# One load of 128 partitions in place of five for the first row tile of a matmul-trace kernel

## The chip, the cores and the metric

The kernel runs on one core of a Trainium2 chip. A core has a matrix engine (TensorE, PE in the profile), three engines for elementwise work (VectorE = DVE, ScalarE = ACT, GpSimd = POOL), SyncE (SP), which here only issues transfers, and 16 DMA engines that move data between the chip's memory (HBM) and the core's on-chip memory (SBUF, 128 partitions). The metric is the device time of one execution in microseconds (us). Where several runs are shown, it is their median.

## The reference

Two stacks of eight 2176 x 2176 float32 matrices are given. For each of the eight pairs the trace of the product is wanted.

```
B, N = 8, 2176
prod = np.matmul(a, b)
traces = np.diagonal(prod, axis1=1, axis2=2).sum(axis=-1)
```

The trace of a product needs no matrix product: it is the sum over i and k of a[i,k] times b[k,i]. So the work is one elementwise product of b with the transpose of a, summed. Both stacks have to be read once, 303 MB in all; there are few operations per byte.

## The kernel before

A matrix is cut into 17 row tiles of 128 rows (`NT`). GpSimd loads them with its own DMA queue, which casts float32 to bfloat16 on the way (`load`, L68 to L78, issue in L76). A load takes eight row tiles at a time (two groups of four, 4352 KB as written), or one single row tile (544 KB). The large loads go to the pool `stage` of three buffers, the single ones to `single` of two. With 17 tiles a matrix takes two large loads and one single one.

Per batch, matrix a is loaded and transposed on TensorE, 128 x 128 at a time (L158 and L179), into PSUM; `evacuate` copies the results into the tile `at`, two of three copies on ScalarE (L115), one on VectorE (L113). Then matrix b is loaded, and VectorE multiplies its rows with the matching rows of `at` and sums in one instruction (`multiply_reduce`, L125). The products of a batch are held behind VectorE's last copy of that batch (`tc.issue_after(copies_end.ins)`, L239). In the last batch a part of the products goes to TensorE (`pe_work`, L286), and the last row tile comes in three pieces (`LAST_PIECES`, L250). At the end VectorE reduces what TensorE has summed, a matmul with ones adds up the partitions, and SyncE writes out eight numbers (L306).

Instructions of one engine run in the order of the program. A load waits for the last reader of the buffer that it overwrites: a large load of a for the transposes of the tile before in that buffer, a large load of b for VectorE's products with the old one.

The first row tile of the first batch is different. It is the single row tile of a (the last 128 rows of the matrix), and is put first in the order of loads. Here `load_first` (L80 to L90) has SyncE load it as float32, without a cast, into the words of a buffer of `stage`. ScalarE casts the left half (L88) and VectorE the right half (L89) into a bfloat16 tile. After this function is called, the first large load of a is issued on GpSimd ahead of the constants (`ahead`, L222), and the identity matrices and other constants follow. The buffer with the float32 words is one of the three of `stage`, so GpSimd's third large load (the first of b) waits until both casts have read it.

The float32 tile is 128 rows of 8704 bytes, 1.11 MB. `FIRST_SPLIT` (L45) cuts it by partitions into five loads:

```
FIRST_SPLIT = [(0, 96), (96, 104), (104, 112), (112, 120), (120, 128)]
```

They are issued one after the other by SyncE (L86, L87). Both casts need all five.

Of the kernel before, what the change touches and what calls it, by code (L numbers as in the profile page):

```python
# [20 lines left out]
def kernel(  # L21
# [6 lines left out]
    nc = tc.nc  # L28
    P = 128
# [12 lines left out]
    a_groups = row_groups(P, even)  # L42
    DOUBLE = 2

    FIRST_SPLIT = [(0, 96), (96, 104), (104, 112), (112, 120), (120, 128)]  # L45

    LAST_PIECES = [(0, 2), (2, 3), (3, 5)]

    const = ctx.enter_context(tc.tile_pool(name="const", bufs=1))
# [30 lines left out]
    def load_first(src, start):  # L80

        words = stage.tile([P, DOUBLE * ROWS, N], bf16, tag="stage")
        plain = words.bitcast(f32).rearrange("p r k -> p (r k)")[:, :N]
        half = N // 2
        t = single.tile([P, 1, N], bf16, tag="single")
        for lo, hi in FIRST_SPLIT:  # L86
            nc.sync.dma_start(out=plain[lo:hi, :], in_=src[start + lo:start + hi, :])  # L87
        nc.scalar.copy(out=t[:, 0, :half], in_=plain[:, :half])  # L88
        nc.vector.tensor_copy(out=t[:, 0, half:], in_=plain[:, half:])  # L89
        return [(start, 1, t)]  # L90
# [119 lines left out]
    for bi in range(BATCH):  # L210
# [8 lines left out]
        for start, m, count in loads:  # L219
            if not tiles:  # L220
                groups = load_first(a[bi], start)
                ahead, issued = load(a[bi], *loads[1])  # L222
                with tc.issue_after(issued.ins):
                    constants()
            elif ahead is not None:
                groups, ahead = ahead, None
            else:
                groups, _ = load(a[bi], start, m, count)
            for start, m, a_t in groups:
                last_transpose = transpose_group(at, a_t, start, m, b_groups)  # L230
# [12 lines left out]
        for start, m, count in joined(b_groups):  # L243
            if last and start == N - P:
# [3 lines left out]
                for g0, g1 in LAST_PIECES:  # L248
                    lo, hi = g0 * WIDE, min(g1 * WIDE, N)
# [29 lines left out]
            out=tiles["sums"][:, bi:bi + 1], in_=acc[:, :cols], axis=mybir.AxisListType.X  # L279
# [4 lines left out]
    with tc.issue_after(last_transpose.ins):  # L284
        for n, (x, y) in enumerate(pe_work):
            nc.tensor.matmul(  # L286
                trace_ps, x, y, start=(n == 0), stop=(n == len(pe_work) - 1),
            )
    late_acc = tiles["late"]
    for n, (x, y) in enumerate(late):  # L290
# [6 lines left out]
        start=True, stop=True,  # L297
    )
    parts = [tiles["sums"][:, BATCH - 1:BATCH]] + [late_acc[:, n:n + 1] for n in range(len(late) + 1)]
    for n, part in enumerate(parts):  # L300
        nc.tensor.matmul(  # L301
            total[:, BATCH - 1:BATCH], tiles["ones"], part,
            start=(n == 0), stop=(n == len(parts) - 1),
# [3 lines left out]
        out=out.rearrange("(a b) -> a b", a=1),  # L307
        in_=tiles["result"][:1, :BATCH],
# [31 lines left out]
```

## Time and profile before

| what | value |
|---|---|
| median of 3 runs | 714.15 us (713.23 to 714.8) |
| the profiled execution | 714.8 us |
| its span, first to last instruction | 713.0 us |
| DVE busy | 411.5 us, 58% of the span |
| PE busy | 206.7 us, 29% |
| ACT busy | 196.9 us, 28% |
| POOL busy | 34.6 us, 5% |
| bytes read from HBM | 303.04 MB, 425 GB/s over the span |
| bytes written by the transfers | 152.32 MB, mean 214 GB/s |

The profile comes from one execution with the hardware profiler on. Its time is 1.8 us above its span: what lies before the first and after the last instruction. Reads are about twice the written bytes because nearly all loads cast four bytes to two. Each line of a timeline has a start, a duration, the engine, the line of the kernel, the operation, what it writes and reads, and in brackets how long the engine was idle before and what ended that. "Landing" of a transfer is the moment at which the engine that waits for it sees it. The trace also holds a record for each DMA packet, with start, duration, queue and bytes written; it does not name the DMA engine that moved it. An instruction queue is a queue by which an engine's program is fetched; it uses the same DMA engines.

Of the transfers, the page lists 16 large loads of a and 15 of b, all issued by GpSimd, with a median of 47.2 and 49.9 us from issue to landing, and for SyncE one load of 816 KB (9.9 us to landing) and four of 68 KB.

### The profile page before, as it was taken

Reading aid. Unit: us, or ns where it says so; the run is one execution under the profiler, and the core shown is the slowest. Engines: PE = TensorE matmul, PEld = TensorE weight load, DVE = VectorE, ACT = ScalarE, POOL = GpSimd, SP = SyncE. Lnnn points to the kernel's source line nnn. Section 1 sums busy time; section 2 is a strip of 40 time slices with the busy share of each in tenths; the row PEclk is TensorE's granted clock in tenths of the full one; section 3 lists DMA queues with packets and bytes.
Section 4 is the critical chain, followed back from the end, with each engine's and each line's share of the span. In section 5 each row is a group of like instructions: output and inputs, shape, how many; then the busy total and the mean of one; then the engine's idle time right before and its main releaser. Section 6 shows DMA issues by size and latency. Waiting matters only on the chain.

```text
span 713.0 us, 3721 instructions
## 1 busy us (share of the span) xinstructions
PE 206.7 (29%) x1406; PEld 193.2 (27%) x1406; DVE 411.5 (58%) x449; ACT 196.9 (28%) x210; POOL 34.6 (5%) x60
## 2 busy tenths in 40 slices
PE   0344005430054200633006420054100651006655
PEld 0344005430054200533006410054100550005545
DVE  0023996229961399514995149942499325993356
ACT  1355003440054300534006330064200652006610
POOL 1000000000000000000001000000000000000000
PEclk9987555775567755767557775576755766557775
DMA  9999999999999999999999999999999999999996
GB/s 195 218 218 215 215 215 217 219 219 209 223 215 216 216 215 222 216 216 216 216 217 218 218 217 216 212 220 217 216 219 212 221 218 216 216 215 219 217 211 122
DMA packets 11652, 152.32 MB, mean 214 GB/s; under 512 B 882, under 2 KB 1138, under 8 KB 3314
## 3 DMA queue, kind: packets, MB, share of 16 engines
q0 software_dynamic: 11456, 150.97, 99.7%
q1 hardware_dynamic: 178, 1.11, 0.7%
q8 instruction: 11, 0.18, 0.1%
q14 instruction: 7, 0.06, 0.0%
HBM read 303.04 MB, written 0.00 MB: 425 GB/s over the span
## 4 chain that ended last, share of the span: by engine, by line
DMA 60%; DVE 31%; issue 7%; PE 2%; DVEq 0%; another core or an unknown queue 0%; POOLq 0%
DMA t<-in_b_dram 50%; DVE scratch L125 30%; DMA t<-in_a_dram 11%; PE ps L158 2%; DVE acc L125 0%; DVEq L125 0%; PE ps L179 0%; PE total L301 0%; DVE result L305 0%; DVE late L125 0%; POOLq L76 0%; DVE sums L278 0%; POOLq L324 0%
## 5 line engine op out<-in xcount | busy, mean ns | idle before, releaser
L125 DVE CUSTOM_DVE_ANT_1 scratch<-at,t 128x2048 bf16<-128x2048 bf16 (+1 forms) x156 | 310.6, 1991 | 73.7 <-DMA t<-in_b_dram 66.4
L115 ACT COPY at<-ps 128x1024 bf16<-128x1024 bf16 x208 | 194.5, 1045 | 467.7 <-PE ps L158 467.6
L158 PE MATMUL ps<-identity,t 128*128 128x128 f32 x1071 | 178.3, 333 | 485.3 <-DMA t<-in_a_dram 310.0
L158 PEld LDWEIGHTS ps<-identity,t 128*128 128x128 f32 x1071 | 166.4, 213 | 493.8 <-DVE sums L278 365.6
L113 DVE COPY at<-ps 128x1024 bf16<-128x1024 bf16 (+2 forms) x104 | 93.6, 902 | 210.1 <-PE ps L158 190.7
L76 POOL DMA_DIRECT2D t<-in_a_dram x23 | 15.3, 663 | 352.9 <-PE ps L179 156.8
L76 POOL DMA_DIRECT2D t<-in_b_dram x26 | 16.8, 646 | 293.0 <-PE ps L179 142.0
L286 PEld LDWEIGHTS <-at 128*128 128x128 bf16 x153 | 17.3, 125 | 13.6 <-issue 13.0
L286 PE MATMUL trace_ps<-t,at 128*128 128x128 bf16 x144 | 16.7, 294 | 12.6 <-DMA t<-in_b_dram 12.6
L179 PE MATMUL ps<-identity,t 128*128 128x128 bf16 x170 | 16.4, 219 | 5.0 <-DVE at L113 4.7
L179 PEld LDWEIGHTS <-t 128*128 128x128 bf16 x170 | 13.0, 100 | 8.4 <-issue 8.2
L125 DVE DVE_READ_ACCUMULATOR2_ANT acc<- 128x1 f32 x163 | 13.3, 82 | 0.0
L89 DVE CAST t<-words 128x1088 bf16<-128x1088 f32 x1 | 0.7, 727 | 13.9 <-DMA words<-in_a_dram 13.9
L88 ACT ACT_TABLE_LOAD x1 | 1.3, 1283 | 14.7 <-DMA words<-in_a_dram 14.7
L250 POOL DMA_DIRECT2D b_t<-in_b_dram x3 | 1.6, 537 | 16.4 <-DVE acc L125 16.4
L125 DVE CUSTOM_DVE_ANT_0 scratch<-at,t 128x128 bf16<-128x128 bf16 x7 | 2.0, 291 | 0.2
L125 DVE CUSTOM_DVE_ANT_1 scratch<-at,b_t 128x256 bf16<-128x256 bf16 (+1 forms) x3 | 1.5, 510 | 0.1
L278 DVE TENSOR_REDUCE sums<-acc 128x1 f32<-128x22 f32 (+1 forms) x8 | 1.4, 174 | 0.3
L286 PE MATMUL trace_ps<-b_t,at 128*128 128x128 bf16 x9 | 1.3, 286 | 0.4 <-DMA b_t<-in_b_dram 0.4
L88 ACT CAST t<-words 128x1088 bf16<-128x1088 f32 x1 | 1.1, 1097 | 0.0
L301 PE MATMUL total<-late,ones 128*1 128x1 f32 x8 | 0.8, 164 | 0.8 <-DVE late L125 0.8
L301 PEld LDWEIGHTS total<-late,ones 128*1 128x1 f32 x8 | 0.3, 80 | 1.2 <-DVE late L125 1.2
(14 smaller groups left out, 2.7 us busy)
## 6 DMA issues: line engine op xcount, KB each, us to landing
t<-in_a_dram POOLq DMA_DIRECT2D x16, 4352.0 KB, 47.2
t<-in_b_dram POOLq DMA_DIRECT2D x15, 4352.0 KB, 49.9
t<-in_b_dram POOLq DMA_DIRECT2D x9, 544.0 KB, 54.4
t<-in_a_dram POOLq DMA_DIRECT2D x7, 544.0 KB, 53.1
t<-in_b_dram POOLq DMA_DIRECT2D x1, 2176.0 KB, 42.3
t<-in_b_dram POOLq DMA_DIRECT2D x1, 1088.0 KB, 26.1
words<-in_a_dram SPq DMA_DIRECT2D x1, 816.0 KB, 9.9
words<-in_a_dram SPq DMA_DIRECT2D x4, 68.0 KB
```

Source lines behind the costliest of these rows:

```text
L76: issued = nc.gpsimd.dma_start(out=part, in_=rows)
L88: nc.scalar.copy(out=t[:, 0, :half], in_=plain[:, :half])
L89: nc.vector.tensor_copy(out=t[:, 0, half:], in_=plain[:, half:])
L113: last_copy = nc.vector.tensor_copy(out=dst, in_=src)
L115: nc.scalar.copy(out=dst, in_=src)
L125: nc.vector.tensor_tensor_reduce(out=out, in0=x, in1=y, scale=1.0, scalar=0.0, op0=MUL, op1=ADD, accum_out=acc,)
L158: nc.tensor.transpose(ps[:, n * m + r, :], words[:, r, c0:c0 + step * (P - 1) + 1:step], tiles[f32],)
L179: last_transpose = nc.tensor.transpose(ps16[:, n, r, :], a_t[:, r, c0:c0 + P], tiles[bf16],)
L250: nc.gpsimd.dma_start(out=row[:, lo:hi], in_=b[bi, start:start + P, lo:hi])
L278: nc.vector.reduce_sum(out=tiles["sums"][:, bi:bi + 1], in_=acc[:, :cols], axis=mybir.AxisListType.X)
L286: nc.tensor.matmul(trace_ps, x, y, start=(n == 0), stop=(n == len(pe_work) - 1),)
L301: nc.tensor.matmul(total[:, BATCH - 1:BATCH], tiles["ones"], part, start=(n == 0), stop=(n == len(parts) - 1),)
```

## The change

The list `FIRST_SPLIT` and its loop go. SyncE issues one load of all 128 partitions. The tile, its buffer, the casts that read it and all else stay as they are.

```diff
-    FIRST_SPLIT = [(0, 96), (96, 104), (104, 112), (112, 120), (120, 128)]
-
     LAST_PIECES = [(0, 2), (2, 3), (3, 5)]
 ...
         t = single.tile([P, 1, N], bf16, tag="single")
-        for lo, hi in FIRST_SPLIT:
-            nc.sync.dma_start(out=plain[lo:hi, :], in_=src[start + lo:start + hi, :])
+        nc.sync.dma_start(out=plain, in_=src[start:start + P, :])
         nc.scalar.copy(out=t[:, 0, :half], in_=plain[:, :half])
         nc.vector.tensor_copy(out=t[:, 0, half:], in_=plain[:, half:])
```

## The prediction

> **What bounds the kernel now.** I read the page's slices and queues first, then the chain that ended last, then the timeline of the first 20 us and of the last 10, and last the trace's records of single DMA packets.
>
> The page (slices: busy tenths, then GB/s; queues: packets, MB, share of 16 engines):
>
> ```profile
> span 713.0 us, 3721 instructions
> DMA  9999999999999999999999999999999999999996
> q0 software_dynamic: 11456, 150.97, 99.7%
> q1 hardware_dynamic: 178, 1.11, 0.7%
> ```
>
> The 16 DMA engines are full from the first slice to the next to last. GpSimd's queue q0 (every load but the first) has work 99.7% of the time; q1 is SyncE's queue, and nearly all of it is the load that the change touches. So the bound is the transfer itself, and a change can only count where it alters when the DMA engines finish. DVE, the busiest compute engine, has 58%.
>
> The end of the chain (start, us, what), and the same place in the timeline:
>
> ```profile
> 677.29 26.12 DMA t<-in_b_dram
> 703.44 0.05 DVEq L125
> ```
>
> ```profile
> 703.45 0.82 PE L286 MATMUL trace_ps<-t,at 128*128 128x128 bf16 x6 [3.50 <-DMA t<-in_b_dram]
> 703.57 2.29 DVE L125 CUSTOM_DVE_ANT_1 scratch<-at,t 128x2048 bf16<-128x2048 bf16 x1 [3.12 <-DMA t<-in_b_dram]
> ```
>
> DVE and PE both stand idle for over 3 us for the load of two row tiles that lands at 703.44. From there DVE runs nearly without a gap to the output, 713.0. That landing sets the end; 9.6 us of tail follow it.
>
> The start (first SyncE's five issues, then what waits for them):
>
> ```profile
> 0.74 1.78 SPq L87 DMA_DIRECT2D words<-in_a_dram  x5
> 1.25 0.82 POOL L76 DMA_DIRECT2D t<-in_a_dram  x1 [0.80 <-POOLq L324]
> ...
> 14.70 1.28 ACT L88 ACT_TABLE_LOAD   x1 [14.70 <-DMA words<-in_a_dram]
> 14.73 0.73 DVE L89 CAST t<-words 128x1088 bf16<-128x1088 f32 x1 [13.86 <-DMA words<-in_a_dram]
> ...
> 17.39 0.72 POOL L76 DMA_DIRECT2D t<-in_b_dram  x1 [13.74 <-ACT t L88]
> ...
> 30.06 6.71 PE L158 MATMUL ps<-identity,t 128*128 128x128 f32 x32 [10.77 <-DMA t<-in_a_dram]
> ```
>
> The casts wait until 14.7 for the split load, and GpSimd's third load waits for ACT's cast to free the buffer. But two loads of 4352 KB are queued by then.
>
> **Engine by engine.** The trace's packet records (start, duration, queue, size, no engine number) can be strung into 16 engines: a packet starts where its predecessor ends. q1 holds 128 packets of 8704 bytes (one row each) and 48 small completion writes, 16 for the load of 96 partitions and 8 for each load of 8. So the large load runs on 16 engines, six rows each; every small one on eight engines, one row each, always the same eight: it is these that carry rows until 12.9 us. Eight engines move ten rows, eight move six.
>
> Completion writes of the first 4352 KB load, per engine in us:
>
> ```
> ten rows: 28.14 28.65 28.68 28.74 28.87 29.05 29.23 29.71   mean 28.88
> six rows: 26.70 27.29 27.35 27.43 27.43 27.65 27.71 27.74   mean 27.41
> ```
>
> The gap of 1.47 is four rows at 0.341 us (the common undisturbed duration in the records), 1.36, and some of four completion writes. Every later load gives each engine the same bytes, in steady packets of 1.302 us, so an engine keeps its lag to the end; it only grows where a packet of the instruction queues is slipped in. Ends: 703.28 to 705.46 for the six-row engines, 705.46 to 706.90 for seven of the ten-row ones, and 708.42 for the engine that was last at 29.71, which I call the late engine. It took four such packets of 8192 bytes (110.7, 281.0, 456.4, 631.8), 0.53 each. Its last packet of the load that ends the wait is at 703.11; DVE sees it at 703.44. So the end hangs on one engine of the ten-row half, 1.5 us behind the next.
>
> **The change, part by part.**
>
> Removed: four of SyncE's five issues. The five took 1.78 us in all, on a queue that holds nothing else until the output at 711.09: worth nothing at the end. Cover: SyncE's idle queue; without it, four issues of 0.3, 1.2 us.
>
> Removed: 32 completion writes on the ten-row half, four per engine, 0.022 us each, overlapping the next packet: at most 0.09, taken into the bounds.
>
> Moved: 32 rows. They were one per engine in turn with GpSimd's packets on eight engines; now all 16 engines have eight rows at the head of their queue. Sum of bytes unchanged. A six-row engine takes two more, at 0.34 undisturbed to 1.2 (rows at 5.5 to 6.4 us lasted 0.9 to 1.2): its end goes from at most 705.46 to at most 707.9. The late engine loses two. Its rows now: six until 5.40, then 0.895 and 1.156, then, each behind a GpSimd packet, 0.895 and 0.488.
> Lower bound of its gain: two undisturbed rows, 2 x 0.341 = 0.68. Upper bound: the very two at the end, 0.895 + 0.488 = 1.38. The engine's own rows speak for the upper end, but the six-row half will then put 16 more rows into the stretch where these were slow, so I take the middle, 1.0.
>
> Does all of it arrive? The late engine at 708.42 - 1.0 = 707.4 should still be last, the others of its half go to 706.2 or below, and a six-row engine at undisturbed prices to 705.46 + 0.68 = 706.1. DVE idles 3.12 us ahead of 703.57, so it can start 1.0 sooner. Behind it the last pieces keep their distance, as they move with the same engine: PE gets the last at 708.77 and is done at 709.2, DVE needs its sum at 710.33. So the whole 1.0 arrives.
>
> The wait of the casts: on one transfer in place of five. It should end sooner, with the last row at some 7.4 us in place of 12.9; completion writes that took up to 3.33 us here can add that. Behind the waiting ACT stand the first evacuations, behind DVE its first copy at 19.33, behind POOL the third load. Worth nothing at the end: the third load's data is not needed by the engines before 47 us, when the second load's packets run out (first engine 47.25), a margin of 30 us on its issue at 17.39; and PE's next work at 30.06 waits for a transfer that was issued at 1.25. That issue and its margin are also the cover if the landing should come later: up to some 12 us more cost only idle time.
>
> [...]
>
> **The sum.** Against the profiled execution, 714.8 (span 713.0 and 1.8 around it): 714.8 - 1.0 = 713.8. The median of the runs is 714.15, 0.65 below the profiled one, so 714.15 - 1.0 = **713.1**, 0.14% less. A measurement of this kernel can tell about 0.2%, 1.4 us, from no change (its runs lie within 713.23 to 714.8), so the likeliest case would hardly be told from none.
>
> **The rivals.**
>
> *The alternation itself makes the late engine late* (0.20). Its lag over its own half grew where rows and GpSimd's packets took turns (0.895 for a row that took 0.35 elsewhere). With one transfer ahead of the queue it would fall to the mean of all 16, 28.15: 29.71 - 28.15 = 1.56, so 712.6, faster. Against: a slow start of this one engine may stay with it in any order.
>
> *The rows get dearer, slower* (0.28). The place is the stretch to 7 us, where 16 engines now read rows together while GpSimd's packets begin. The late engine's ten rows cost 3.6 for the first six (1.79 to 5.40) and 0.895 + 1.156 + 0.895 + 0.488 = 3.4, together 7.0; it decides against the change when eight cost over 7.0 + 1.4 = 8.4, 1.06 each. For it: rows at 1.8 to 3.2 us took 0.7 to 1.1, those at 5.5 to 6.4 0.9 to 1.2, GpSimd's first packets 2.1 in place of 1.3. Against: rows between lasted 0.33 to 0.6. At 1.12 each: 9.0 - 7.0 = +2.0, so 716.1.
>
> *Nothing* (0.10): the late engine's lag is set by GpSimd's first packets and the instruction packets alone, or a second engine inherits the place: 714.1.
>
> The forecast has 0.36, of which 0.22 stay within 0.2% and 0.14 pass it, given a margin of 0.7 in the medians. The remaining 0.06 are instruction packets that fall on other engines (steps of 0.53 or 1.1): 0.03 faster, 0.01 same, 0.02 slower.
>
> **How the numbers follow.** Faster by over 0.2%: 0.14 + 0.20 + 0.03 = 0.37. Within: 0.22 + 0.10 + 0.01 = 0.33. Slower: 0.28 + 0.02 = 0.30. The forecast's own range is 714.15 - 1.38 to 714.15 - 0.68, 712.8 to 713.5. The range for 8 in 10 goes down to 1.56 plus the medians' margin of 0.7, 711.9, and up to the dear rows at 716.1: 711.9 to 716.2.
>
> **What would show it.** Right: SyncE with one issue; 16 completion writes on q1 for the load and rows on all engines equally; the casts near 8 to 11 us in place of 14.7 and GpSimd's third issue near 11; the first 4352 KB load landing near 29.0 in place of 30.02; DVE's last wait ending near 702.4 in place of 703.44. Wrong: the first load lands at 30 or later (dear rows); another engine, of the other half, ends last; or the last wait moves by over 1.4 though the first landing moved less, which would point at instruction packets.

## The result, and the profile after

The changed kernel takes 711.14 us (median of 6 runs, 710.94 to 711.24) against 714.12 (6 runs, 713.23 to 714.8). The ratio is 0.9958 with a 95% interval of 0.9945 to 0.9971: 3.0 us less, three times the forecast's 1.0, and below the lower end of its range, 711.9. The two profiled executions, on which the rest is worked out, are 3.66 apart (714.8 and 711.14), as the one of before was the slowest of its runs.

The page of the changed kernel, its span and its two queues of loads (packets, MB, share of 16 engines), and the end of its chain:

```profile
span 709.4 us, 3709 instructions
q0 software_dynamic: 11456, 150.97, 100.1%
q1 hardware_dynamic: 146, 1.11, 0.4%
```

```profile
674.06 25.69 DMA t<-in_b_dram
699.75 0.03 issue
```

```profile
699.79 4.23 PE L283 MATMUL trace_ps<-t,at 128*128 128x128 bf16 x36 [3.50 <-DMA t<-in_b_dram]
699.91 2.29 DVE L122 CUSTOM_DVE_ANT_1 scratch<-at,t 128x2048 bf16<-128x2048 bf16 x1 [3.09 <-DMA t<-in_b_dram]
```

Nothing has changed places: PE and DVE still stand idle for over 3 us until the load of two row tiles lands, and DVE runs to the end from there. Only the landing has moved, from 703.44 to 699.75, 3.69, and with it the span, 3.6. The same bytes cost SyncE's queue 0.4% of the engines' time in place of 0.7%.

The start of the changed kernel:

```profile
0.74 0.40 SPq L84 DMA_DIRECT2D words<-in_a_dram  x1
...
5.70 1.10 ACT L85 CAST t<-words 128x1088 bf16<-128x1088 f32 x1 [3.68 <-DMA words<-in_a_dram]
5.70 0.73 DVE L86 CAST t<-words 128x1088 bf16<-128x1088 f32 x1 [4.83 <-DMA words<-in_a_dram]
...
7.09 0.71 POOL L74 DMA_DIRECT2D t<-in_b_dram  x1 [3.45 <-ACT t L85]
...
26.32 6.29 PE L155 MATMUL ps<-identity,t 128*128 128x128 f32 x32 [17.31 <-DMA t<-in_a_dram]
```

The casts start at 5.70 in place of 14.7, 9.0 sooner, and that by itself is worth nothing: PE, done with the first tile, then waits 17.31 us instead of 10.77. What counts is the last line: the first 4352 KB load lands at 26.32 in place of 30.06, 3.7 sooner, and this 3.7 is kept to the end.

Where it came from is seen in two windows (from:to, length, busy time of the engines, TensorE's clock, DMA share, GB/s), the kernel before first and the changed one after it:

```profile
3.00:5.00 2.00, 0.00 (x0) 0.00 (x0) 0.00 (x0) 0.00 (x0) 0.65 (x1) 1.00 1.06 270
5.00:8.00 3.00, 0.00 (x0) 0.00 (x0) 0.00 (x0) 0.00 (x0) 0.00 (x0) 1.00 1.19 163
```

```profile
3.00:5.00 2.00, 0.00 (x0) 0.00 (x0) 0.00 (x0) 0.00 (x0) 0.65 (x1) 1.00 1.06 431
5.00:8.00 3.00, 1.06 (x5) 1.09 (x6) 0.73 (x1) 1.10 (x1) 0.71 (x1) 1.00 1.27 270
```

The DMA engines are as busy in the one as in the other (1.06), but move 270 GB/s in the one and 431 in the other. Busy engines that move two thirds of the bytes are held up by something else. The packet records agree: rows that begin between 3.0 and 4.5 us last 0.579 us (median) in the kernel before and 0.328 in the changed one; the small loads' rows at 5.3 to 7 us 0.83 to 1.22, and GpSimd's packets beside them 1.9 (up to 2.6) in place of 1.30. A packet of GpSimd is one of its 17408-byte writes, undisturbed at 1.30.

Strung into engines as in the prediction, the completions of the first 4352 KB load are, in us:

```
before: 26.70 to 29.71, mean 28.15, the last 1.56 behind the mean
after:  25.49 to 25.99, mean 25.78, the last 0.21 behind the mean
```

So the mean of all engines moved by 2.37, and the spread about it shrank by 1.35: 3.72 for the last one. The packet durations add up to the first of these: SyncE's rows took 4.58 us per engine (mean of 16) before and 3.12 after, 1.46 less, and the 256 packets of GpSimd's first load 21.80 and 20.90, 0.90 less. At the end the last packets are done at 708.42 and 704.79, 3.63 apart.

### The profile page after: what moved, and what is told of

Its sections match the earlier page's. It is cut to its first block, busy times and chain, and to the rows that moved or that the text cites. A ratio compares the mean times of both kernels' runs of the same rounds, so it can differ in the third digit from the quotient of the medians.

```text
span 709.4 us, 3709 instructions
## 1 busy us (share of the span) xinstructions
PE 206.3 (29%) x1406; PEld 193.0 (27%) x1406; DVE 411.4 (58%) x449; ACT 196.8 (28%) x210; POOL 34.6 (5%) x60
## 4 chain that ended last, share of the span: by engine, by line
DMA 56%; DVE 34%; issue 7%; PE 2%; another core or an unknown queue 2%; POOL 0%; DVEq 0%; POOLq 0%
DMA t<-in_b_dram 43%; DVE scratch L122 33%; DMA t<-in_a_dram 13%; PE ps L155 1%; DVE acc L122 0%; DVEq L122 0%; PE ps L176 0%; POOL identity masks.py:199 0%; DVE at L110 0%; POOL identity masks.py:197 0%; PE total L298 0%; DVE result L302 0%; DVE late L122 0%; POOLq L74 0%
```

## The experiments

Each edit is shown against the changed kernel, without its indentation. "Complete" is the completion, per engine, of GpSimd's first 4352 KB load.

Theory P, the author's assumption from these durations (0.579 and 0.328 for the same row): where several DMA engines write into neighbouring partitions at once, they hold each other up, as if they shared a write path about as fast as one engine. Loads of 96, 64, 32, 16 and 8 neighbouring partitions make the engines meet in this way, a load of all 128 does not. "Meet" stands for that below, and a "write path" in the expectations is part of the assumption: the records show how long a row took, not such a path. The rivals: the number of loads, their size, the uneven share of rows, the side that reads.

**Only the 96 partitions.**

```diff
-nc.sync.dma_start(out=plain, in_=src[start:start + P, :])
+for lo, hi in [(0, 96), (96, 128)]:
+    nc.sync.dma_start(out=plain[lo:hi, :], in_=src[start + lo:start + hi, :])
```

> Two loads, of 96 and of 32 partitions, in place of the kernel before's 96 and four times 8. All 16 DMA engines then move eight rows each and nothing is small. Theory P (engines that write into partitions of the same few groups share a write path that is about as fast as one engine): the 96 stay as slow as in the kernel before, 0.54 to 0.60 us a row against 0.328 in the kernel after, the 32 are no faster; some 2 us lost on every engine, first 4352 KB load complete at 27.5 to 28.2 on all engines within about 0.8 us, time 712.6 to 713.4. Rival S (the loads of 8 partitions are the whole cost, by their size or by the uneven share of rows): rows at 0.33, first load complete near 25.8, time 711.1.

Measured: 713.08 us (ratio to the kernel before 0.9983, 0.9973 to 0.9992). Rows of 0.536 (median, 3.0 to 4.5 us), first 4352 KB load complete at 26.80 to 28.22. Time and rows are close to what theory P gave; the completions start earlier than its 27.5 and spread over 1.4 us in place of 0.8. Rival S falls: the small loads of 8 are not the whole cost. Every engine has eight rows here, and still some 1.9 us of the gain are gone. The first window moves no more than that of the kernel before:

```profile
3.00:5.00 2.00, 0.00 (x0) 0.00 (x0) 0.00 (x0) 0.00 (x0) 0.65 (x1) 1.00 1.02 270
```

**Two loads of 64.** 

```diff
-nc.sync.dma_start(out=plain, in_=src[start:start + P, :])
+for lo, hi in [(0, 64), (64, 128)]:
+    nc.sync.dma_start(out=plain[lo:hi, :], in_=src[start + lo:start + hi, :])
```

> Two loads of 64 partitions each. Theory P: each load reaches only a part of the write paths with all 16 engines, so rows cost about twice 0.328, 0.66 us, in both; 8 x 0.33 = 2.6 us lost on every engine, first 4352 KB load complete at 28 to 28.5, time 713.3 to 714. [...] Rival U (96 is slow because its six rows per engine divide badly, not for the partitions that it reaches): 64 divides evenly, rows at 0.33, time 711.1.

Measured: 711.92 us (0.9964, 0.9951 to 0.9977), first load complete at 26.10 to 27.94. The time misses theory P's range, and the records show why. The factor of two in the expectation was the author's estimate; the first 64 rows cost 0.685, 2.1 times 0.328, but GpSimd's packets begin at 4.0, ahead of the second 64 rows. These come one by one between GpSimd's packets, from 5.3 us on at 0.341 each, and no longer meet. In these records it takes both, neighbouring partitions and the same moment. Rival U falls: 64 divides evenly, and its rows were slower than those of 96.

**Five loads cut by columns.**

```diff
-nc.sync.dma_start(out=plain, in_=src[start:start + P, :])
+for lo, hi in [(0, 1632), (1632, 1768), (1768, 1904), (1904, 2040), (2040, 2176)]:
+    nc.sync.dma_start(out=plain[:, lo:hi], in_=src[start:start + P, lo:hi])
```

> Five loads again, but cut by columns: each has all 128 partitions, the first three quarters of the columns and the others a sixteenth each. Theory P: every load reaches all write paths, so nothing is lost but the packets' own overhead: first 4352 KB load complete at 25.7 to 26.3, time 711.0 to 711.5. Rival C (five loads on SyncE's queue in place of one cost the time by their number): first load complete near 28, time 713 to 714.

Measured: 711.62 us (0.9959, 0.9944 to 0.9974), first load complete at 25.87 to 27.08, packets of 6528 bytes at 0.248, the same rate as 8704 in 0.328. It is 0.12 above the range that theory P gave, three engines complete past its 26.3, and it is far from what rival C asks. Five loads cost 0.5 us, not 3. That is the narrow packets' own price: 544 bytes take 0.041 us, 32 of them per engine, and with these SyncE's packets take 3.65 us per engine in place of 3.12. But the load lands very late:

```profile
40.69 0.73 DVE L87 CAST t<-words 128x1088 bf16<-128x1088 f32 x1 [39.82 <-DMA words<-in_a_dram]
```

VectorE's half of the tile is there at 40.69, in place of 5.70, as the narrow packets come one by one between GpSimd's packets until 39. Nothing at the end of this kernel hangs on that, as the 0.5 is no more than the packets' price.

**One engine made late.**

```diff
 nc.sync.dma_start(out=plain, in_=src[start:start + P, :])
+spare = words.bitcast(f32).rearrange("p r k -> p (r k)")[:, N:2 * N]
+nc.sync.dma_start(out=spare[0:17, :], in_=src[start:start + 17, :])
```

> The kernel after, with one more SyncE load of 17 rows into unused words (nobody reads them). 17 partitions do not divide over engines, so all 17 rows should fall on one DMA engine, 17 x 0.33 = 5.6 us for it alone. Theory E (the kernel ends with its slowest DMA engine, and a lag of the start is kept to the end): one engine completes the first 4352 KB load near 31, the other 15 near 25.8; the end moves by 5.6 less that engine's own slack, 0 to 2.7 us (engines end between 702.1 and 704.8 in the kernel after), so time 714.0 to 716.8. Rival M (the bytes count in sum, 148 KB over 16 engines): 0.35 us, time 711.5.

Measured: 714.46 us, just the time of the kernel before (1.000, 0.999 to 1.001). Fifteen engines complete the first 4352 KB load at 25.60 to 25.92, one at 31.37: 17 rows of 0.33. The lines of this run that show it (the second is the wait at the end):

```profile
28.40 0.72 POOL L74 DMA_DIRECT2D t<-in_b_dram  x1 [24.74 <-DMA words<-in_a_dram]
...
703.13 2.29 DVE L124 CUSTOM_DVE_ANT_1 scratch<-at,t 128x2048 bf16<-128x2048 bf16 x1 [3.18 <-DMA t<-in_b_dram]
```

GpSimd's third load is issued at 28.40, 21 us later than in the changed kernel, as its buffer is in use by the extra rows; the engines have work without it (the packets strung into engines leave no gap over 0.04 us from 14 to 690 us). The landing at the end is 3.2 later than the changed kernel's. The late engine's last packet is done at 707.95, 3.2 after the changed kernel's last one; without its 17 rows, 5.6 us, it would have been done at 702.4 by estimate, early among the engines, which is its slack of 2.4. Theory E holds, rival M (711.5) does not: 148 KB of 303 MB, on one engine of 16, undo the whole change.

**The four small loads of 8 alone.** They are added to the changed kernel, into words that nobody reads.

```diff
 nc.sync.dma_start(out=plain, in_=src[start:start + P, :])
+spare = words.bitcast(f32).rearrange("p r k -> p (r k)")[:, N:2 * N]
+for lo in range(96, 128, 8):
+    nc.sync.dma_start(out=spare[lo:lo + 8, :], in_=src[start + lo:start + lo + 8, :])
```

> The kernel after, with the kernel before's four loads of 8 partitions added, into unused words (nobody reads them). Theory P: eight engines write into the same 8 partitions, rows of 0.9 to 1.2 us where they meet, GpSimd's packets beside them stretched as in the kernel before (2.1 in place of 1.3). Eight engines complete the first 4352 KB load at 28 to 29 in place of 25.8, the others near 26.5; time 713.3 to 714.3. Rival I (only the uneven share counts: four rows more at 0.33 to 0.34): eight engines at 27.2, the others at 25.8; time 711.6 to 712.5.

Measured: 713.04 us (0.9979, 0.9970 to 0.9989), between both expectations. Eight engines complete the first load at 27.90 to 28.66, the others at 26.22 to 26.72; six of the rows took 0.97 to 1.18 and GpSimd's packets at 5 to 7 us 1.71 (up to 2.05). So the engines meet as theory P says, but once only, and then take turns with GpSimd's packets at 0.34: the price was set too high.

**Eight loads of 16, and four of 32.**

```diff
-nc.sync.dma_start(out=plain, in_=src[start:start + P, :])
+for lo, hi in [(0, 16), (16, 32), (32, 48), (48, 64), (64, 80), (80, 96), (96, 112), (112, 128)]:
+    nc.sync.dma_start(out=plain[lo:hi, :], in_=src[start + lo:start + hi, :])
```

```diff
-nc.sync.dma_start(out=plain, in_=src[start:start + P, :])
+for lo, hi in [(0, 32), (32, 64), (64, 96), (96, 128)]:
+    nc.sync.dma_start(out=plain[lo:hi, :], in_=src[start + lo:start + hi, :])
```

> Eight loads of 16 partitions in place of one of 128: each engine has one row of each. Theory P: 16 engines write into 16 neighbouring partitions, so a row costs as much as in the loads of 8, 0.9 to 1.3 us, where the engines meet; some three loads before GpSimd's packets begin, the rest in turn with these; first 4352 KB load complete at 28.5 to 32, time 713.8 to 717.5. Rival S2 (nothing but the loads of 96 and of 8 is slow, 64 having cost only 0.8 us): rows at 0.33 to 0.66, first load complete near 26.5, time 711.5 to 712.

> Four loads of 32 partitions. Theory P: the write paths are set by the partitions that a load reaches. If 32 neighbouring partitions reach as many as 64, a row costs 0.66 to 0.70 us as in the two loads of 64, first 4352 KB load complete at 26.7 to 27.5, time 711.9 to 712.8. If they reach half as many, 1.3 us a row, first load complete at 28 or later, time above 713.3. [...]

Measured: the loads of 16 714.55 us (0.9998, 0.9989 to 1.0008), rows of 1.056 (the third load; those of the first lasted 0.33 to 0.55, which is not explained), first load complete at 27.60 to 29.61, earlier in part than the 28.5 expected; the loads of 32 712.53 us (0.9972, 0.9961 to 0.9983), rows of 0.666, complete at 26.66 to 28.22, two engines past the 27.8 of the others; four rows took 1.2 to 1.8, for no reason that a run shows. With the loads of 16 most of the lost time lies in GpSimd's packets: the 256 of its first load take 23.07 us per engine in place of 20.90, while the rows take 4.31 in place of 3.12. The first windows of the runs with 64 and with 16 (columns as above; both hold packets of GpSimd from 4.0 and 3.8 us on, so the loads are better told apart by the rows):

```profile
3.00:5.00 2.00, 0.00 (x0) 0.00 (x0) 0.00 (x0) 0.00 (x0) 0.65 (x1) 1.00 1.30 252
```

```profile
3.00:5.00 2.00, 0.00 (x0) 0.00 (x0) 0.00 (x0) 0.00 (x0) 0.65 (x1) 1.00 1.26 183
```

Row durations by the partitions of a load, with all 16 engines at work: 128: 0.328, 96: 0.53 to 0.58, 64: 0.69, 32: 0.67, 16: 1.06. That 32 cost no more than 64 while 16 cost over three times as much as 128 does not fit a rule of "fewer is slower"; why the durations step in this way is not shown. Of the two cases expected for the loads of 32 the rows give the first, 0.67 beside 0.69 for 64. For the load of 96 no run placed its rows so that the engines would not meet; that they meet there is argued from the other loads, not shown.

**The side that reads.**

```diff
-nc.sync.dma_start(out=plain, in_=src[start:start + P, :])
+nc.sync.dma_start(out=plain[0:96, :], in_=src[0:96 * 22 - 21:22, :])
+nc.sync.dma_start(out=plain[96:128, :], in_=src[5:5 + 32 * 60 - 59:60, :])
```

> The two loads of 96 and 32 partitions again, but the rows are read from all over the matrix (every 22nd and every 60th) in place of 128 neighbouring rows; the first row tile then holds other rows, so the first batch's sum is not that of the reference. Theory P (the cost is on the side that writes): rows stay at 0.55 to 0.6 us, first 4352 KB load complete at 26.8 to 28.3, time 712.4 to 713.7. Rival H (the reads from HBM meet, as neighbouring rows are read at once): rows at 0.33, first load complete near 25.8, time 711.1 to 711.6.

Measured: 712.04 us (0.9965, 0.9952 to 0.9978), rows of 0.526, first load complete at 26.41 to 27.20. The rows of the 96 stay slow, so rival H falls for them. The time and the earliest completions lie below the ranges that theory P gave: the late rows, which begin at 5.5 to 6.5 us and belong to the 32 behind the 96, took 0.62 (median) here and 0.87 with neighbouring rows. Only the reads differ between the two kernels (the kernel before took 714.46 beside the one and 714.45 beside the other), so the reads, or what hangs on them, have a part in the price: 0.6 us of mean completion (27.43 and 26.79), and 1.0 of the 1.9 us in the time (713.08 and 712.04). How they act was not tried further and stays open.

**The same small loads, 12 partitions apart**, beside the changed kernel on the same chip.

```diff
 nc.sync.dma_start(out=plain, in_=src[start:start + P, :])
+spare = words.bitcast(f32).rearrange("p r k -> p (r k)")[:, N:2 * N]
+for lo in range(4):
+    nc.sync.dma_start(out=spare[lo:lo + 85:12, :], in_=src[start + 96 + 8 * lo:start + 104 + 8 * lo, :])
```

> The kernel after, once more, so that it stands beside the next run on the same chip: 711.1 to 711.3, first 4352 KB load complete at 25.5 to 26.0.

> The kernel after with four more loads of 8 rows into unused words, as in the run that added the kernel before's four small loads, but the 8 partitions of a load lie 12 apart in place of side by side. Theory P: what costs is that several DMA engines write into neighbouring partitions at once; 12 apart they do not meet, so only the uneven share of rows is left: rows at 0.33 to 0.34, GpSimd's packets at 1.30, eight engines complete the first 4352 KB load at 27.2, the others at 25.8; time 711.6 to 712.5. [...] Rival S3 (loads of 8 partitions are slow by their size, wherever they go): as with neighbouring partitions, rows of 1.0 to 1.2, GpSimd's packets to 2.0, eight engines at 27.9 to 28.7, the others at 26.2 to 26.7, time 713.0.

Measured: the changed kernel again 711.06 us (0.9954, 0.9937 to 0.9970), complete at 25.65 to 25.94; the loads 12 apart 712.35 us (0.9969, 0.9959 to 0.9980). Eight engines complete at 27.09 to 27.30, the others at 25.87 to 26.16. Rows from 5.3 to 7 us took 0.34. The window of 5 to 8 us, first with the 8 side by side, then 12 apart:

```profile
5.00:8.00 3.00, 0.33 (x2) 0.35 (x3) 0.73 (x1) 1.10 (x1) 0.00 (x0) 1.00 1.26 200
```

```profile
5.00:8.00 3.00, 0.93 (x5) 0.96 (x6) 0.73 (x1) 1.10 (x1) 0.00 (x0) 1.00 1.17 270
```

Same rows, same size, same number of loads and engines; only the partitions differ. 200 GB/s become 270, the rows that meet no longer take up to 1.18, and GpSimd's packets are back at 1.30 (median). That partitions 12 apart would not meet was the author's assumption; rows of 0.34 show it for these loads. So for loads of 8 it is shown that neighbouring partitions cost, as theory P has it, though not by what path, and rival S3 falls. What is left here is the uneven share alone.

**The account.** Taking medians against the changed kernel (711.06 to 711.14): four rows more on eight engines 712.35 - 711.06 = 1.3; eight engines meeting in 8 partitions 713.04 - 712.35 = 0.7; the load of 96, with that of 32 behind it, 713.08 - 711.14 = 1.9. In the kernel before, the eight engines carry not four but two rows more than in the changed one (ten against eight), so of the first term half counts, 0.65, an estimate. Together 3.3, against the 3.0 (first runs) to 3.5 (714.55 - 711.06) of the whole change. The agreement is rough: the third term holds a load of 32 that the kernel before does not have, and it was 0.9 with far rows (712.04 - 711.14). No run was faster than the changed kernel, and none points at a version that would be.

## Why the prediction was wrong, point by point

*What bounds the kernel*: right. The end hung on the landing at 703.44, that on one DMA engine's lag, and that on the first 13 us; the run with 17 rows on one engine shows these steps (5.6 us of lag, 3.2 of them at the landing, the rest that engine's slack), and in the changed kernel all of the shift arrived at the end as argued (3.72 at the first load, 3.69 at the landing).

*Removed issues and completion writes, the earlier casts, the third load*: worth nothing, as said. A third load 21 us later (28.40) did not starve the engines. That the landing was not on the path was right. It came 9.0 sooner. Measured from the first issue, two loads of 64 landed after 13.4 us (14.16 - 0.74), five by columns after 40.0 (40.69 - 0.74), the five of the kernel before after 14.0 (14.70 - 0.74). In all three the last packets came in turn with GpSimd's, and that set the landing more than the number of loads.

*Moved rows*: this is the step that failed. It read the slow rows, 0.9 to 1.2 us at 5.5 to 6.4, as a property of that stretch of time, into which 16 more rows would come, and let the six-row engines pay for two rows more ("its end goes from at most 705.46 to at most 707.9"). The slowness came with the removed loads, a price that the prediction did not have in its sum: with one load of 128 the first one or two rows of each engine are slow (0.4 to 1.29 us, before 2.6), and of those that follow none lasts over 0.396. And the six-row engines got earlier too (27.41 to 25.78 in the mean) though they carry a third more rows. The last engine's gain was bounded at 1.38 by two of the late engine's own rows; it was 3.72, since other rows and the first GpSimd packets had been stretched as well. What the prediction did count, two rows fewer on the late half, is worth some 0.65 by the run with loads 12 apart (half of its 1.3), near the lower bound of 0.68. So the forecast "faster" rests on a true but small term; some 2.3 of the 3.0 come from the term it lacked, what rows and GpSimd's packets cost where engines meet.

The sign that could have been read: from 3.3 to 5.1 us rows lasted 0.51 to 0.68, on all 16 engines at once and before GpSimd had a packet under way, with 0.328 on record for the same packet at 2.9 (why those few were fast is not explained). The 270 GB/s from 3 to 5 us, with engines 1.06 busy, against the 425 GB/s read over the whole span, say the same: only uncast rows move in that window, as many bytes written as read.

*The rivals*: that the alternation made one engine late had the right sign, and it too took the mean of 28.15 as fixed. Its mechanism is refuted: rows in turn with GpSimd's packets cost 0.341 where the engines do not meet (loads of 64, loads 12 apart). The dearer rows, the rival of the other sign, were exactly wrong: they got cheaper.

*The range*: its lower end, 711.9, came from that rival's 1.56 and 0.7 for the medians. No case in it let all engines gain at once. A slip of the sum for the dear rows, 8.4 / 8 = 1.05 and not 1.06, changes nothing.

## What to carry to other kernels

When every DMA engine is busy and the GB/s of a window fall well below those of a steady one (270 from 3 to 5 us here, against the 425 read over the whole span), ask where the packets go before putting it down to the time of the run: compare one packet size's duration in both. Load all 128 partitions at once: a row took 0.328 so, and 0.53 to 1.06 in loads of 96 to 16. A cut by columns kept the rate of the wide packets here (0.248 for 6528 bytes), but its narrow pieces behind another queue's packets landed at 40.69 in place of 5.70, so it is for data that can wait. In this kernel, which is bound by transfers and whose every later load gives all engines the same bytes, none evened out a lag of the start: 3.72 us at the first load were 3.69 at the landing near the end. A small transfer on a part of the engines cost its time there less their slack, not its share of the bytes: four rows on eight engines 1.3 us, 17 rows on one 3.3.

## What the runs showed of the hardware that was not expected

Most kernels whose engines meet also scatter more from run to run: 713.31 to 714.98 for the kernel before (20 runs), 713.46 to 715.01 with loads of 16, 712.39 to 713.61 with 96 and 32; where they do not meet, 710.94 to 711.24 (the changed kernel, 10 runs), 712.21 to 712.43 (12 apart), 714.31 to 714.61 (17 rows on one engine). It is no rule: with 96 and 32 far rows, which meet, the runs lay within 712.02 to 712.47, by columns, which do not, within 711.43 to 711.82. 17 partitions went to one single engine (complete at 31.37, the others by 25.92), and meeting rows stretched GpSimd's own packets as well, from 1.30 to as much as 2.6 us in the kernel before.
